# A hybrid decoder layer: Delta-net masks and scalings moved from POOL to DVE, small inverse products spaced out, a weight load moved ahead of the masks

## The chip, the cores and the metric

The kernel runs on one core of one Trainium2 chip. The metric is the device time of one execution in microseconds (us). Three timed executions of the kernel before gave a median of 1263.71 us (1262.24 to 1264.34). The engines are called as in the profile: PE (matrix products; PEld is its weight load), DVE (vector), ACT (scalar and activations), POOL (the third elementwise engine), SP (here it only issues transfers).

## The reference

One decoder layer over 16 meta tokens and 256 tokens, width 2048, in float32. The input goes through an RMS norm and one combined projection. Half of its columns feed a differential attention, the other half a gated Delta net; both results are concatenated, projected back and added; then comes a SwiGLU feed-forward of hidden width 5632. The part that matters here is the Delta net, in chunks, for each of 8 heads:

```python
diff = gc[..., :, None] - gc[..., None, :]
decay = jnp.where(incl, jnp.exp(jnp.where(incl, diff, 0.0)), 0.0)
kb = kc * bc[..., None]
lmat = jnp.where(strict, jnp.einsum('bhnid,bhnjd->bhnij', kb, kc) * decay, 0.0)
tmat = lmat + jnp.eye(CHUNK, dtype=f32)
u = lax.linalg.triangular_solve(tmat, vc * bc[..., None], left_side=True, lower=True,
                                unit_diagonal=True)
qk = jnp.einsum('bhnid,bhnjd->bhnij', qc, kc) * decay
...
o = rmsnorm(o, o_norm_w) * jax.nn.silu(z.reshape(B, L, DN_HEADS, DN_DV).astype(f32))
```

`decay` is the exponential of a difference of running sums of the gates, masked to a triangle; the key products are scaled by `bc` (beta and the key norms) and by the decay; a unit triangular matrix is inverted for each head.

## The kernel before, in words

**Weights.** Every weight matrix streams from HBM as tiles of 128 x 1024 floats (`raw`, 512 KB, four buffers). Each is split by ACT into a rounded part `hi` (line 250) and by DVE into the remainder `lo` (line 251); each has four buffers. The products then run in a fast format as `hi*xh + hi*xl + lo*xh` (line 1086 in the input projection, 24 products per tile; line 1133 afterwards). `next_w` splits four tiles ahead and asks for loads three further. The input itself is split the same way at the start, into `xh` (ACT, line 325) and `xl` (DVE, line 326), 16 slices of 128 x 272, with the first weight tiles split between the slices.

**Side work.** `proj` emits the weight products in groups of six and, after each group, `tasks.step()` advances up to two of the waiting generators (`decay`, `conv_task`, `unit`, `inverses`, `attention` ...). A generator's `yield n` postpones it by n such steps. So the distance of two pieces of side work on PE is written in steps, not in time. ACT and SP run their instructions in the order in which they are emitted; on PE, DVE and POOL a scheduler puts them in order, by its own estimate of times, when the program is built. Once built, every engine takes its instructions strictly in that order. PSUM tiles of the side work come from a ring of four (`aux`), so the fifth user waits until the first is read.

**The Delta net.** `meta_block` treats the 16 meta positions of all heads as one 128 x 128 block; `unit(g, n)` treats four heads of one of two 128-position chunks (four units). Each starts with `decay`: a mask times the gates (line 475, POOL), products with a triangle (line 479, PE), an exponential (ACT), a mask (line 485, POOL). When the key scalars `c1` (line 573) and `c2` (line 574) are there, POOL scales the decay by `c1` (line 792) and DVE multiplies it with the key products of line 795 into `gT` (line 798; line 735 for the meta block). The keys are scaled by `c2` on POOL (line 815). `inverses(n)` inverts the triangles: it sends `gT` through DRAM, runs a recursion on 16 x 16 blocks on DVE (lines 630, 631), fetches the result, and joins blocks to 32, 64 and 128 with small PE products (lines 663, 677: 32 products of 32 x 16, or 16 of 32 x 32, on parts of the PE array). For that POOL masks `gT` into `gm` (line 624). `meta_block` then makes the first state: line 749 transposes the values (PE), line 753 scales them (DVE), line 763 multiplies them by the inverse (PE), line 759 scales keys for eight heads (POOL), line 772 makes the state (PE). `z_task` applies the SiLU gate (ACT) and the output norm weight (line 911, POOL).

**The key path early on.** `conv_task` scales a finished projection (line 502, DVE), convolves it (line 511 on ACT, three passes of line 514 on DVE per head) and applies SiLU (ACT) into `k_c`, `v_c`, `q_c`. `sums` transposes the keys on PE (line 539).

Of the kernel before, what the change touches and what calls it, by code (L numbers as in the profile page):

```python
# [15 lines left out]
P = 128  # L16
# [139 lines left out]
def layer(tc, xT, aw, x, w_in, w_ba, w_out, w_gate, w_up, w_down, cmask, dist, par, out):  # L156
# [122 lines left out]
        elif i in (3, 5, 7):  # L279
            load_to((i + 1) // 2)  # L280
    wba_raw = wk.tile([P, KT, WBA], F32, name="wba_raw")
    nc.sync.dma_start(out=wba_raw, in_=w_ba)
    cmsk = const.tile([P, len(CM), P], F32, name="cmsk")
    nc.sync.dma_start(out=cmsk, in_=cmask)
    par_sb = const.tile([P, NPAR], F32, name="par_sb")
    nc.sync.dma_start(out=par_sb, in_=par)
    dist_sb = wk.tile([P, META + P + T], F32, name="dist_sb")

    def pr(n):
# [33 lines left out]
    for k in range(KT):  # L323
        src, w = xr[k // 8][:, k % 8, :], aw_sb[:, k:k + 1]
        S.activation(xh[:, k, :], src, AF.Copy, scale=w)
        V.scalar_tensor_tensor(xl[:, k, :], src, w, xh[:, k, :], ALU.mult, ALU.subtract)  # L326
        if k == 0:
            split_to(1, 2)
        elif k in (5, 9, 13):
            split_to((k + 3) // 4)  # L330


    rbc = const.tile([P, T], F32, name="rbc")
# [138 lines left out]
    def decay(u, gcols, tri, m, dst):  # L472
        yield at_least("ga", 1)
        gt = yield from r2.get(m, P)
        G.tensor_tensor(gt, bc_mid(mk("tri_s"), m), bc_last(gcols, P), ALU.mult)
        yield 3
        ps = yield from aux.get(m, P)
        for h in range(m):
            PE.matmul(ps[:, h, :], gt[:, h, :], mk("tri_i"), start=True, stop=True)
        r2.free()  # L480
        yield 1
        act(dst, ps, AF.Exp)
        aux.free()
        yield 1
        G.tensor_tensor(dst, dst, bc_mid(tri, m), ALU.mult)
        mark("decay")


# [44 lines left out]
    ktm = {}  # L533
# [71 lines left out]
    def inverses(n):  # L605

        m0, m = (0, 9) if n == 0 else (9, 8)
        f = slice(1 + 8 * n, 9 + 8 * n)
        q = 8 * m
        yield at_least(f"gT{n}", 3 - n)
        gT, y, gm = big_tile("gT"), big_tile("y"), big_tile("gm")
        d = dpool.tile([m, PLANE], F32, tag=f"d{n}", name=f"d{n}")
        nc.sync.dma_start(out=d[:, 0:P * P].rearrange("m (r c) -> r m c", c=P), in_=gT[:, m0:m0 + m, :])
        gb = (yield from r1.get(16, 16))[0:q]
        nc.sync.dma_start(out=gb, in_=bass.AP(d.tensor, d.offset, [[PLANE // 8, q], [P, 16], [1, 16]]))  # L620
        yt = yield from r1.get(256)
        V.memset(yt, 0.0)
        V.memset(yt[:, 0:256:17], 1.0)
        G.tensor_tensor(gm[:, f, :], gT[:, f, :], bc_mid(mk("off16"), 8), ALU.mult)
        yb = yt[0:q].rearrange("p (r i) -> p r i", i=16)
        tb = (yield from r1.get(16, 16))[0:q]
        yield 14
        for i in range(1, 16):
            t = tb[:, 0:i, 0:i]
            V.tensor_tensor(t, yb[:, 0:i, 0:i], bc_mid(gb[:, 0:i, i], i), ALU.mult)  # L630
            V.tensor_reduce(yb[:, 0:i, i], t, AX.X, ALU.add, negate=True)  # L631
            if i > 4:
                yield 3
        V.tensor_copy(tb, yb.rearrange("p r i -> p i r"))
        e = dpool.tile([q, 256], F32, tag=f"e{n}", name=f"e{n}")
        nc.sync.dma_start(out=e, in_=tb.rearrange("p i r -> p (i r)"))
        x16 = yield from r1.get(m, 16)
        nc.sync.dma_start(out=x16, in_=bass.AP(e.tensor, e.offset, [[16, P], [2048, m], [1, 16]]))
        r1.free(3)
        yield 14  # L640
        x32 = yield from r2.get(m, 32)
        V.tensor_scalar(x32[:, :, 0:16], x16, pr("lo16"), None, ALU.mult)
        V.tensor_scalar(x32[:, :, 16:32], x16, pr("hi16"), None, ALU.mult)
        r1.free()
        y32 = yield from r2.get(m, 32)
        V.transpose(y32, x32)
        if n == 0:
            expand(y[:, 0:1, :], y32[:, 0:1, :], 1, 32, mk("bd32"))
            mark("inv_m")
        yield 2  # L650
        if n == 0:
            x32, y32 = x32[:, 1:9, :], y32[:, 1:9, :]
        gT, y, gm = gT[:, f, :], y[:, f, :], gm[:, f, :]
        a_ = yield from r2.get(8, 64)
        for w in (16, 32):

            parts = [(32 * b, 32 * b) for b in range(4)] if w == 16 else [(0, 32), (64, 96)]
            src = gm if w == 16 else gT
            ps = yield from aux.get(8, w)

            for h in range(8):
                for r0, c0 in parts:
                    PE.matmul(ps[c0:c0 + 32, h, :], src[r0:r0 + 32, h, c0:c0 + 32], x32[r0:r0 + 32, h, 0:w],
                              start=True, stop=True, tile_position=(r0, c0))
            yield 2
            a = a_[:, :, 0:w]
            if w == 16:
                S.copy(a, ps)
            else:
                for _, c0 in parts:  # L670
                    S.copy(a[c0:c0 + 32], ps[c0:c0 + 32])
            aux.free()
            yield 1
            ps = yield from aux.get(8, w)
            for h in range(8):
                for _, c0 in parts:
                    PE.matmul(ps[c0:c0 + 32, h, :], y32[c0:c0 + 32, h, :], a[c0:c0 + 32, h, :],
                              start=True, stop=True, tile_position=(c0, c0))
            yield 2
            if w == 16:  # L680
                V.tensor_tensor(x32[:, :, 0:16], x32[:, :, 0:16], ps, ALU.subtract)
                aux.free()
                V.transpose(y32, x32)
                yield 2
        x64 = a_
        for b in range(4):
            bs = slice(32 * b, 32 * b + 32)
            if b % 2:
                V.tensor_scalar(x64[bs, :, 0:32], ps[bs], -1.0, None, ALU.mult)
            else:  # L690
                G.tensor_copy(x64[bs, :, 0:32], x32[bs])
        aux.free()
        V.tensor_scalar(x64[:, :, 32:64], x32, pr("hi32"), None, ALU.mult)
# [24 lines left out]
        yield 2  # L718
        S.activation(y[0:64, :, 64:128], ps[0:64], AF.Copy, scale=-1.0)
        aux.free()  # L720
        r2.free(2)
        mark("inv")
        mark(f"inv{n}")

    state = wk.tile([P, H, P], F32, tag="state", name="state")
    def meta_block():
# [28 lines left out]
        for g in range(2):  # L755
            t = yield from r2.get(4, P)
            ksm.append(t)
            for h in range(4):
                G.tensor_scalar(t[:, h, :], ktm["m"], c2m[:, 4 * g + h:4 * g + h + 1], None, ALU.mult)
        aux.free()  # L760
        yield 1
        ps = yield from aux.get(1, P)
# [17 lines left out]
    def unit(g, n):  # L780
# [8 lines left out]
        yield from decay(u, ga[:, cs], mk("tri_i"), 4, dq)  # L789
        yield at_least("c1", 1)  # L790
        kc = qkv["k"]
        G.tensor_tensor(dq, dq, bc_last(c1[:, cs], P), ALU.mult)
        ps = yield from aux.get(4, P)
        for i, h in enumerate(hs):
            PE.matmul(ps[:, i, :], kc[:, h, ts_], kc[:, h, ts_], start=True, stop=True)
        yield 3
        yield 1
        V.tensor_tensor(dt, ps, dq, ALU.mult)
        aux.free()
        yield 1  # L800
        mark(f"gT{n}")
# [10 lines left out]
        aux.free()  # L812
        if n == 0:
            ks = ktm[g]
            G.tensor_tensor(ks, ks, bc_last(c2[:, cs], P), ALU.mult)
        yield at_least(f"state{g}", n + 1)
        ps = yield from aux.get(4, P)
        for i, h in enumerate(hs):
# [24 lines left out]
        for i, h in enumerate(hs):  # L843
            PE.matmul(ps[:, i, :], kc[:, h, ts_], qc[:, h, ts_], start=True, stop=True)
        yield 1
        V.tensor_tensor(dq, ps, dq, ALU.mult)
        aux.free()
        if n == 0:
            ps = yield from aux.get(4, P)
# [35 lines left out]
        r2.free()  # L885
        yield 1
        val = yield from r2.get(4, P)
        V.tensor_tensor(val, ps, sz[:, 4 * g:4 * g + 4, P * n:P * (n + 1)], ALU.mult)
        aux.free()
        yield at_least("chain", 4)  # L890
        for part in ("hi", "lo"):
# [11 lines left out]
    def z_task(h, ps):  # L903
# [2 lines left out]
        V.tensor_tensor(z, ps[:, 0:SEQ], rbc[:, META:T], ALU.mult)  # L906
        mm.free()
        yield 1
        act(z, z, AF.Silu)
        yield 1  # L910
        G.tensor_scalar(sz[:, h, :], z, pr("onorm"), None, ALU.mult)
        r1.free()
        mark("z")

# [419 lines left out]
```

## Time and profile before

| what | value |
|---|---|
| median of 3 timed runs | 1263.71 us (1262.24 to 1264.34) |
| the profiled execution's own time | 1262.79 us |
| its span, first to last instruction | 1261.0 us |
| PE busy | 1244.4 us (99%) |
| DVE busy | 729.4 us (58%), 1084 instructions |
| ACT busy | 610.9 us (48%) |
| POOL busy | 46.8 us (4%), 48 instructions |
| PE clock granted, mean | 0.996 |

The busy times are sums over instructions as the profiler saw them; a PE product that waits inside the pipeline counts as busy, so PE's 99% does not say that PE ran at its best speed throughout. The idle times that the profile lists before each instruction, with what ended them, say where PE stood still. Windows of the span show each engine's busy time and the clock granted to PE in that stretch: 1.00 is full speed, 0.50 half. Times of single instructions are from their start to their end; where instructions of one engine overlap in its pipeline, a row of n of them is shorter than n times one.

### The profile page before, as it was taken

Reading aid. Unit: us, or ns where it says so; the run is one execution under the profiler, and the core shown is the slowest. Engines: PE = TensorE matmul, PEld = TensorE weight load, DVE = VectorE, ACT = ScalarE, POOL = GpSimd, SP = SyncE. Lnnn points to the kernel's source line nnn. Section 1 sums busy time; section 2 is a strip of 40 time slices with the busy share of each in tenths; the row PEclk is TensorE's granted clock in tenths of the full one; section 3 lists DMA queues with packets and bytes.
Section 4 is the critical chain, followed back from the end, with each engine's and each line's share of the span. In section 5 each row is a group of like instructions: output and inputs, shape, how many; then the busy total and the mean of one; then the engine's idle time right before and its main releaser. Section 6 shows DMA issues by size and latency. Waiting matters only on the chain.

```text
span 1261.0 us, 18878 instructions
## 1 busy us (share of the span) xinstructions
PE 1244.4 (99%) x7469; PEld 1092.2 (87%) x7469; DVE 729.4 (58%) x1084; ACT 610.9 (48%) x962; POOL 46.8 (4%) x48
## 2 busy tenths in 40 slices
PE   8999999999999999999999999999999999999998
PEld 7998989999999988888888888888888888888886
DVE  7789956567676666645544554554455454544443
ACT  6664454466776655544344444444444433343332
POOL 0322200110000000000000000000000000000000
PEclk9999999999999999999999999999999999999999
DMA  8456642345544655566665566556666555656562
GB/s 270 134 168 176 179 138 85 118 151 167 158 144 151 218 167 183 177 194 191 190 190 190 187 192 192 184 186 198 185 189 194 187 191 190 215 189 213 191 210 83
DMA packets 150280, 224.31 MB, mean 178 GB/s; under 512 B 11560, under 2 KB 72368, under 8 KB 149936
## 3 DMA queue, kind: packets, MB, share of 16 engines
q1 hardware_dynamic: 150192, 223.11, 55.8%
q8 instruction: 58, 0.95, 0.3%
q14 instruction: 30, 0.25, 0.1%
HBM read 219.73 MB, written 3.35 MB: 177 GB/s over the span
## 4 chain that ended last, share of the span: by engine, by line
PE 89%; DVE 6%; ACT 2%; DMA 1%; issue 1%; SPq 0%; DVEq 0%; ACTq 0%
PE mm L1133 64%; PE mm L1086 19%; DVE lo L251 2%; DVE r L514 1%; DMA raw<-in_w_in_dram 1%; PE aux L1216 1%; PE aux L1034 1%; ACT hi L250 1%; PE aux L989 1%; DVE r L630 0%; PE aux L1021 0%; PE aux L381 0%; SPq L276 0%; DVE r L631 0%; DMA e<-r 0%
## 5 line engine op out<-in xcount | busy, mean ns | idle before, releaser
L251 DVE TENSOR_TENSOR lo<-raw,hi 128x1024 fp32r<-128x1024 f32 (+1 forms) x409 | 504.9, 1236 | 469.5 <-ACT hi L250 468.4
L250 ACT CAST hi<-raw 128x1024 fp32r<-128x1024 f32 (+1 forms) x409 | 428.8, 1050 | 546.7 <-PE mm L1133 447.7
L1133 PE MATMUL mm<-hi,uh 128*128 128x512 f32 x704 | 274.9, 390 | 0.0
L1133 PE MATMUL mm<-hi,ul 128*128 128x512 f32 x704 | 274.0, 389 | 0.0
L1133 PE MATMUL mm<-lo,uh 128*128 128x512 f32 x704 | 273.9, 389 | 0.0
L1086 PE MATMUL mm<-xh,hi 128*128 128x272 f32 (+2 forms) x896 | 260.7, 291 | 1.6 <-ACT hi L250 1.6
L1086 PE MATMUL mm<-xh,lo 128*128 128x272 f32 (+2 forms) x896 | 255.6, 286 | 3.0 <-issue 1.8
L1086 PE MATMUL mm<-xl,hi 128*128 128x272 f32 (+2 forms) x896 | 256.7, 287 | 0.0
L1133 PE MATMUL mm<-hi,hT 128*128 128x512 f32 x704 | 217.2, 389 | 0.0
L1086 PEld LDWEIGHTS mm<-xh,hi 128*128 128x128 f32 x896 | 169.6, 189 | 5.8 <-issue 3.0
L1086 PEld LDWEIGHTS mm<-xh,lo 128*128 128x128 f32 x896 | 168.8, 189 | 1.9 <-DVE lo L251 1.9
L1086 PEld LDWEIGHTS mm<-xl,hi 128*128 128x128 f32 x896 | 169.3, 189 | 0.3 <-DVE xl L326 0.2
L1133 PEld LDWEIGHTS mm<-hi,ul 128*128 128x128 f32 x704 | 132.1, 188 | 27.6
L1133 PEld LDWEIGHTS mm<-hi,hT 128*128 128x128 f32 x704 | 132.1, 188 | 27.3
L1133 PEld LDWEIGHTS mm<-hi,uh 128*128 128x128 f32 x704 | 132.2, 188 | 27.1
L1133 PEld LDWEIGHTS mm<-lo,uh 128*128 128x128 f32 x704 | 132.2, 188 | 27.0
L1133 PE MATMUL mm<-lo,hT 128*128 128x512 f32 x352 | 136.9, 389 | 0.0
L1133 PEld LDWEIGHTS mm<-lo,hT 128*128 128x128 f32 x352 | 66.1, 188 | 13.7
L514 DVE SCALAR_TENSOR_TENSOR r<-r,par_sb,r 128x272 f32<-128x272 f32 (+1 forms) x72 | 34.7, 541 | 0.2 <-ACT r L511 0.2
L1133 PE MATMUL mm<-hi,mix_d_hi 128*128 128x512 f32 x64 | 25.5, 399 | 0.0
L1133 PE MATMUL mm<-hi,mix_a_hi 128*128 128x512 f32 x64 | 25.1, 392 | 0.0
L1133 PE MATMUL mm<-hi,mix_d_lo 128*128 128x512 f32 x64 | 25.0, 390 | 0.0
(305 smaller groups left out, 849.8 us busy)
## 6 DMA issues: line engine op xcount, KB each, us to landing
raw<-in_w_in_dram SPq DMA_DIRECT2D x111, 512.0 KB, 3.6
raw<-in_w_gate_dram SPq DMA_DIRECT2D x88, 512.0 KB, 3.5
raw<-in_w_up_dram SPq DMA_DIRECT2D x88, 512.0 KB, 3.5
raw<-in_w_down_dram SPq DMA_DIRECT2D x88, 512.0 KB, 3.5
raw<-in_w_out_dram SPq DMA_DIRECT2D x32, 512.0 KB, 3.5
xr<-in_xT_dram SPq DMA_DIRECT2D x7, 272.0 KB, 6.0
x_k_c<-in_x_dram SPq DMA_DIRECT2D x1, 1024.0 KB, 6.5
x_q_c<-in_x_dram SPq DMA_DIRECT2D x1, 1024.0 KB
```

What stands on the lines that cost most here:

```text
L250: S.copy(hi[:, js], raw[:, js])
L251: V.tensor_tensor(lo[:, js], raw[:, js], hi[:, js], ALU.subtract)
L514: V.scalar_tensor_tensor(acc, raw[:, off + j:off + j + m], cwv[:, ct, j:j + 1], acc, ALU.mult, ALU.add)
L989: PE.matmul(pss[m][:, cut[n]], q[ms, P * n:P * (n + 1)], k[ms, 0:NK[n]], start=True, stop=True)
L1034: PE.matmul(po[:, n, :], l, r, start=(j == 0), stop=(j == 1 + n))
L1086: PE.matmul(acc[c][:, 0:n], a[:, k, cs], b[:, kt, t0:T], start=(kt == 0 and i == 0), stop=(kt == KT - 1 and i == 2))
L1133: PE.matmul(acc[b], l, r[:, i % 2, :], start=(first and i == 0 and j == 0), stop=(last and i == len(kts) - 1 and j == 2))
L1216: PE.transpose(pst[:, j, :], g_[:, P * j:P * (j + 1)], ident)
```

## The change

1. `decay`: the mask times gates (line 475) becomes one `tensor_scalar` per head on DVE, 17 of them of 128 x 128; the mask after the exponential (line 485) goes from POOL to DVE as it is.
2. `unit`: the scaling of the decay by `c1` (line 792, POOL) goes. Instead `c1` is folded into the two products that use the decay (lines 798 and 846): each DVE instruction over 128 x 512 becomes four over 128 x 128 with three operands.
3. `inverses`: the mask of line 624 goes to DVE. The waits between the small products grow from 2, 1 and 2 steps to 5, 3 and 5.
4. Key scaling: line 759 goes to DVE as it is (eight instructions); line 815 becomes eight instructions of 128 x 128 on DVE.
5. `z_task` writes the SiLU straight to `sz`; the output norm weight of line 911 moves into the later product of line 888.
6. At the start, the first tiles are split in two halves each, one input slice earlier, and the fifth weight tile's load is issued ahead of the loads of `w_ba`, the masks (640 KB) and the parameters.

```diff
     wba_raw = wk.tile([P, KT, WBA], F32, name="wba_raw")
-    nc.sync.dma_start(out=wba_raw, in_=w_ba)
     cmsk = const.tile([P, len(CM), P], F32, name="cmsk")
-    nc.sync.dma_start(out=cmsk, in_=cmask)
     par_sb = const.tile([P, NPAR], F32, name="par_sb")
-    nc.sync.dma_start(out=par_sb, in_=par)
...
         if k == 0:
             split_to(1, 2)
-        elif k in (5, 9, 13):
-            split_to((k + 3) // 4)
+            load_to(5)
+            for dst, src in ((wba_raw, w_ba), (cmsk, cmask), (par_sb, par)):
+                nc.sync.dma_start(out=dst, in_=src)
+        elif k in (4, 8, 12):
+            split_to(k // 4 + 1, 2)
+            load_to(k // 4 + 5)
...
-        G.tensor_tensor(gt, bc_mid(mk("tri_s"), m), bc_last(gcols, P), ALU.mult)
+        for h in range(m):
+            V.tensor_scalar(gt[:, h, :], mk("tri_s"), gcols[:, h:h + 1], None, ALU.mult)
...
-        G.tensor_tensor(dst, dst, bc_mid(tri, m), ALU.mult)
+        V.tensor_tensor(dst, dst, bc_mid(tri, m), ALU.mult)
...
-        G.tensor_tensor(gm[:, f, :], gT[:, f, :], bc_mid(mk("off16"), 8), ALU.mult)
+        V.tensor_tensor(gm[:, f, :], gT[:, f, :], bc_mid(mk("off16"), 8), ALU.mult)
...
-            yield 2
+            yield 5
             a = a_[:, :, 0:w]
...
-            yield 1
+            yield 3
             ps = yield from aux.get(8, w)
...
                 V.transpose(y32, x32)
-                yield 2
+                yield 5
...
-                G.tensor_scalar(t[:, h, :], ktm["m"], c2m[:, 4 * g + h:4 * g + h + 1], None, ALU.mult)
+                V.tensor_scalar(t[:, h, :], ktm["m"], c2m[:, 4 * g + h:4 * g + h + 1], None, ALU.mult)
...
-        G.tensor_tensor(dq, dq, bc_last(c1[:, cs], P), ALU.mult)
...
-        V.tensor_tensor(dt, ps, dq, ALU.mult)
+        for i in range(4):
+            V.scalar_tensor_tensor(dt[:, i, :], ps[:, i, :], c1[:, cs][:, i:i + 1], dq[:, i, :], ALU.mult, ALU.mult)
...
-            G.tensor_tensor(ks, ks, bc_last(c2[:, cs], P), ALU.mult)
+            for i in range(4):
+                V.tensor_scalar(ks[:, i, :], ks[:, i, :], c2[:, cs][:, i:i + 1], None, ALU.mult)
...
-        act(z, z, AF.Silu)
-        yield 1
-        G.tensor_scalar(sz[:, h, :], z, pr("onorm"), None, ALU.mult)
+        act(sz[:, h, :], z, AF.Silu)
```

The product of line 846 (`qkT`) is split into four like that of line 798, and that of line 888 gets the norm weight as a third operand.

The scheduler puts PE's and DVE's instructions in a new order in three places that matter below. In the listings, `L` is the source line (from line 281 on, a line of the changed kernel differs by a few from that of the kernel before: 1086 is 1087, 539 is 541, 479 is 481, 663 is 665, 677 is 679, 763 is 765, 753 is 755), then the operation, out<-in, and the size of the result.

PE, early in the key path. `L539` are the key transposes of `sums`, two heads at a time, into two PSUM tiles; `L1086` are weight products. Before:

```order
L539 MATMUL aux_749<-cmsk,k_c 128x128 x2
L1086 MATMUL mm_615<-xh,hi_567 128x272
...
L539 MATMUL aux_730<-cmsk,k_c 128x128
L539 MATMUL aux_749<-cmsk,k_c 128x128
```

Now:

```order
L541 MATMUL aux_767<-cmsk,k_c 128x128 x2
L1087 MATMUL mm_633<-xh,hi_573 128x272
...
L1087 MATMUL mm_633<-xh,hi_635 128x272
L541 MATMUL aux_748<-cmsk,k_c 128x128
L541 MATMUL aux_767<-cmsk,k_c 128x128
```

Between the transposes of the first two heads and those of the next two there were four weight products; now there are 19.

DVE, where the meta block's first state is prepared. `L753` scales the transposed values, `L514` is the convolution, `L681` belongs to the small inverse products. Before:

```order
L514 SCALAR_TENSOR_TENSOR r_54_1989<-r_52_1979,par_sb,r_54_1989 128x256
L251 TENSOR_TENSOR lo_2004<-raw_1901,hi_2003 128x1024
L753 TENSOR_SCALAR r_56_2105<-aux_2096,ksq 128x128
L251 TENSOR_TENSOR lo_2085<-raw_1931,hi_2084 128x1024
L681 TENSOR_TENSOR r_16_2015<-r_16_2015,aux_2117 128x8x16
```

Now:

```order
L516 SCALAR_TENSOR_TENSOR r_54_2015<-r_52_2005,par_sb,r_54_2015 128x256
L251 TENSOR_TENSOR lo_2030<-raw_1927,hi_2029 128x1024
L761 TENSOR_SCALAR r_21_2132<-ktm_m,c2m 128x128 x4
L761 TENSOR_SCALAR r_22_2137<-ktm_m,c2m 128x128 x4
L755 TENSOR_SCALAR r_56_2130<-aux_2122,ksq 128x128
L251 TENSOR_TENSOR lo_2111<-raw_1957,hi_2110 128x1024
```

The eight key scalings (line 759 before, 761 now) stand ahead of the scaling of the values.

PE, at the small inverse products (`L663`, `L677`; x32 is one group) and the meta block's products. Before:

```order
L663 MATMUL aux_2036<-r_16_2015,gm 32x16 x32
...
L749 MATMUL aux_2096<-cmsk,r_55_2075 128x128
...
L677 MATMUL aux_2117<-r_18_2035,r_17_2018 32x16 x32
...
L763 MATMUL aux_2156<-r_56_2105,y 128x128
L663 MATMUL aux_2159<-r_19_2079,gm 32x16 x32
...
L772 MATMUL aux_2214<-r_57_2198,r_21_2107 128x128 x4
```

Now:

```order
L665 MATMUL aux_2062<-r_16_2041,gm 32x16 x32
...
L751 MATMUL aux_2122<-cmsk,r_55_2101 128x128
...
L665 MATMUL aux_2143<-r_19_2105,gm 32x16 x32
...
L765 MATMUL aux_2182<-r_56_2130,y 128x128
...
L774 MATMUL aux_2205<-r_57_2190,r_21_2132 128x128 x4
L541 MATMUL aux_2210<-cmsk,q_c 128x128 x4
...
L679 MATMUL aux_2244<-r_18_2061,r_17_2044 32x16 x32
```

The dots are weight products. Three groups of 32 small products stood before the state products of line 772 (774 now). Now two stand there, and the third comes after them, 24 weight products and both halves of the state later than the product of line 763.

More of the change, by code (lines that the diff above doesn't have):

```diff
@@ L795, in unit @@
             PE.matmul(ps[:, i, :], kc[:, h, ts_], kc[:, h, ts_], start=True, stop=True)
-        yield 3
-        yield 1
-        V.tensor_tensor(dt, ps, dq, ALU.mult)
+        yield 4
+        for i in range(4):
+            V.scalar_tensor_tensor(dt[:, i, :], ps[:, i, :], c1[:, cs][:, i:i + 1], dq[:, i, :], ALU.mult, ALU.mult)
         aux.free()
@@ L845, in unit @@
         yield 1
-        V.tensor_tensor(dq, ps, dq, ALU.mult)
+        for i in range(4):
+            V.scalar_tensor_tensor(dq[:, i, :], ps[:, i, :], c1[:, cs][:, i:i + 1], dq[:, i, :], ALU.mult, ALU.mult)
         aux.free()
@@ L887, in unit @@
         val = yield from r2.get(4, P)
-        V.tensor_tensor(val, ps, sz[:, 4 * g:4 * g + 4, P * n:P * (n + 1)], ALU.mult)
+        V.scalar_tensor_tensor(val, ps, pr("onorm"), sz[:, 4 * g:4 * g + 4, P * n:P * (n + 1)], ALU.mult, ALU.mult)
         aux.free()
@@ L908, in z_task @@
         yield 1
-        act(z, z, AF.Silu)
-        yield 1
-        G.tensor_scalar(sz[:, h, :], z, pr("onorm"), None, ALU.mult)
+        act(sz[:, h, :], z, AF.Silu)
         r1.free()
```

## The prediction

> **What bounds the kernel now.** I read the page's totals first, then the chain that ended last. The first row of the next fence is the span, the second PE's total, the third the chain by engine.
>
> ```profile
> span 1261.0 us, 18878 instructions
> PE 1244.4 (99%) x7469; PEld 1092.2 (87%) x7469; DVE 729.4 (58%) x1084; ACT 610.9 (48%) x962; POOL 46.8 (4%) x48
> PE 89%; DVE 6%; ACT 2%; DMA 1%; issue 1%; SPq 0%; DVEq 0%; ACTq 0%
> ```
>
> PE sets the end. Its products stay the same in number and size, so only time in which PE stands still, or runs at half clock, can be won. The list of PE's waits, grouped by what ended them, gives the places that this change can touch.
>
> ```profile
> PE aux L795 <- DVE gT L735: 3.1, 1, 3.1
> PE mm L1086 <- issue: 1.8, 1, 1.8
> PE aux L539 <- ACT k_c L196: 1.7, 1, 1.7
> PE mm L1086 <- ACT hi L250: 1.6, 2, 0.9
> ```
>
> Then I cut the span into windows around these waits: length, busy time (and instructions) of PE, PEld, DVE, ACT and POOL, granted clock, DMA share, GB/s.
>
> ```profile
> 9.10:12.40 3.30, 1.85 (x13) 1.43 (x12) 1.91 (x3) 2.62 (x5) 0.00 (x0) 1.00 1.06 380
> 89.20:161.20 72.00, 68.93 (x611) 68.50 (x609) 69.44 (x156) 32.73 (x46) 21.39 (x21) 0.98 0.61 175
> 95.30:98.30 3.00, 0.00 (x0) 0.00 (x0) 3.00 (x5) 0.67 (x2) 0.88 (x1) 0.91 0.00 0
> 98.40:101.10 2.70, 2.70 (x12) 2.70 (x13) 2.70 (x5) 1.02 (x2) 1.60 (x1) 0.50 0.87 263
> 162.70:166.00 3.30, 1.69 (x72) 1.46 (x71) 0.68 (x2) 0.27 (x1) 0.78 (x2) 1.00 0.90 286
> 166.20:169.40 3.20, 3.20 (x16) 3.20 (x16) 1.23 (x1) 1.21 (x2) 0.00 (x0) 0.50 0.04 12
> ```
>
> Two readings. After the waits at 95 and at 164 the clock is 0.50 for about 3 us, although PE is busy: a stall there is paid again, with half of 2.70 = 1.35 us and half of 3.20 = 1.6 us. It did not follow at 9.1, where PE was idle for 3.30 - 1.85 = 1.45 us, and it did at 162.7, with 1.61 idle. And DVE is busy for 69.44 of 72 us between 89 and 161: there the second engine has no room.
>
> **The first tiles.** Three more splits in halves cost ACT time: two halves take 1.34 us, one whole 1.05.
>
> ```profile
> 4.75 1.34 ACT L250 CAST hi<-raw 128x512 fp32r<-128x512 f32 x2 [0.30 <-DMA raw<-in_w_in_dram]
> 17.45 2.28 ACT L340 ACTIVATE r<-xr 128x544 f32<-128x544 f32 x4
> 20.50 1.05 ACT L250 CAST hi<-raw 128x1024 fp32r<-128x1024 f32 x1 [0.76 <-DVE lt L426]
> 24.59 0.40 ACT L375 CAST wba<-wba_raw 128x256 fp32r<-128x256 f32 x1
> ```
>
> A first half is ready 1.05 - 0.67 = 0.38 us sooner, at the two waits for `hi` of the list; against that stand 0.29 us more of ACT time for each split. I take 0.2 us gained. The fifth tile's earlier load gives nothing: its split at 20.50 stands behind ACT's own queue (line 340), not behind a DMA. On SP the masks, `w_ba` and parameters go behind 512 KB, an estimated 1.4 us at the 380 GB/s of the 9.1 row; `w_ba` is first used at 24.59 with no wait for it. If that cover fails, up to 1.4 is lost; from a clock drop there about the same, and at best I see 0.5 gained.
>
> **The wait at 52.5.** POOL's masks (line 475) leave; 17 instructions go to DVE, ahead of the split and of the convolution for which `k_c` waits.
>
> ```profile
> 40.43 0.17 DVE L404 COPY ga<-bat 128x16 f32<-128x16 f32 x1
> 40.51 0.17 DVE L405 COPY gb<-bat 128x16 f32<-128x16 f32 x1
> 46.23 0.18 DVE L449 SCALAR_TENSOR_TENSOR ga<-ga,t 128x17 f32<-128x17 f32 x1
> 46.49 5.38 POOL L475 TENSOR_TENSOR r<-cmsk,ga 128x128 f32<-128x128 f32 x5 [46.06 <-DVE ga L449]
> 50.89 3.54 DVE L514 SCALAR_TENSOR_TENSOR r<-r,par_sb,r 128x272 f32<-128x272 f32 x6
> 66.27 2.55 DVE L514 SCALAR_TENSOR_TENSOR r<-r,par_sb,r 128x272 f32<-128x272 f32 x6
> 54.53 0.44 PE L539 MATMUL aux<-cmsk,k_c 128*128 128x128 f32 x2 [1.72 <-ACT k_c L196]
> 203.50 1.90 DVE L822 SCALAR_TENSOR_TENSOR r<-aux,ne_gc,r 128x128 f32<-128x128 f32 x7
> 160.89 0.34 DVE L753 TENSOR_SCALAR r<-aux,ksq 128x128 f32<-128x128 f32 x1
> ```
>
> While POOL works, DVE's instructions are longer: six of line 514 take 3.54 us against 2.55 in the later row. A `tensor_scalar` of 128 x 128 with POOL idle is not in the trace. Bounds, start to start: 0.08 us (lines 404 to 405, 16 columns) and 1.90/7 = 0.27 (line 822, the same size with two operands, one in PSUM); above that 0.34, start to end of line 753. I take 0.18, midway between the first two. So DVE ends line 514 at 46.41 + 17 x 0.18 + 0.2 (line 466) + 1.2 (line 251) + 2.55 = 53.4 us instead of 54.4. The second transposes of line 539 move behind 15 more weight products; products stand 68.93/611 = 0.113 us apart on average in the 89.2 row, so 1.7 us. PE gets there at 52.8 + 1.7 - 0.2 = 54.3 instead of 54.53 - 1.72 = 52.8, later than `k_c` is ready. The wait of 1.7 goes, 1.8 us with its restart; at 0.27 DVE ends at 54.9 and 0.7 of it is lost. The mask of line 485 adds five DVE instructions, four of 128 x 512 of which none costs more than a split's 1.2 us; DVE waits for ACT there:
>
> ```profile
> 57.77 1.48 DVE L251 TENSOR_TENSOR lo<-raw,hi 128x1024 fp32r<-128x1024 f32 x1 [2.21 <-ACT hi L250]
> ```
>
> Its cover is that idle time; without it a few us of DVE come due in the stretch from 89 on.
>
> **The wait at 95.** The fourth unit's products need the PSUM tile that line 735 reads.
>
> ```profile
> 89.43 4.36 POOL L792 TENSOR_TENSOR qkT<-qkT,c 128x512 f32<-128x512 f32 x4 [10.76 <-DVE c L573]
> 89.61 1.01 DVE L574 TENSOR_TENSOR c<-c,eg 128x17 f32<-128x17 f32 x1
> 90.55 1.13 DVE L731 TENSOR_SCALAR gT<-gT,c 128x128 f32<-128x128 f32 x1
> 91.60 4.88 DVE L514 SCALAR_TENSOR_TENSOR r<-r,par_sb,r 128x272 f32<-128x272 f32 x4
> 97.95 0.28 DVE L735 TENSOR_TENSOR gT<-aux,gT 128x128 f32<-128x128 f32 x1
> ```
>
> Line 514 took 4.88 us for four, at the pace of 66.27 1.7; lines 574 and 731 took 2.14, by the rows of lines 449 and 753 about 0.54. That is 3.2 + 1.6 = 4.8 us, more than the wait of 3.1, and line 735 moves up with it. The wait goes, and the half clock: 3.1 + 1.35 = 4.4 us (3.1 to 4.6).
>
> **The wait at 164.** Nothing that the profile shows held PE here. What remains is instruction supply: the DMA view for 152.9 to 163.9 has no line of the instruction queue q8; for 163.9 to 166.1 it has the first of these rows. The second is the page's for the whole span.
>
> ```profile
> q8 instruction: 1, 0.02, 2.7%
> q8 instruction: 58, 0.95, 0.3%
> 166.19 0.38 PE L1086 MATMUL mm<-xh,lo 128*128 128x260 f32 x1 [1.80 <-issue]
> ```
>
> One block is 0.95 MB/58 = 16 KB. Three groups of 32 small products run here in quick succession, and weight loads go with them, so PE uses up instructions much faster than among weight products; the next block came too late. With the waits of 5, 3 and 5 steps one group moves behind the state products. I take the stall and its half clock as gone: 1.8 + 1.6 = 3.4 us (0 to 3.4). The Trainium skill, "Runtime: NRT & Kernel Launch", section "Instruction fetch mechanics", says that instructions come in blocks of 256 (16 KiB), fetched while the current one runs, and that crossing a block's end is mostly hidden; by that the stall is something else, or spacing won't move it, and the sum below would be smaller by the 3.4 us. The trace agrees on the block's size and not, here, on the hiding; that it doesn't go is a rival.
>
> **The new wait, at line 763.** Before line 753 DVE now has eight key scalings of line 759 and more. What POOL's work cost DVE between 89 and 161 comes back:
>
> ```profile
> L251 DVE TENSOR_TENSOR lo<-raw,hi 128x1024 fp32r<-128x1024 f32 x21 | 29.2, 1392 | 0.5 <-ACT hi L250 0.5
> L798 DVE TENSOR_TENSOR gT<-aux,qkT 128x512 f32<-128x512 f32 x4 | 2.6, 676 | 0.0
> 159.76 1.21 DVE L251 TENSOR_TENSOR lo<-raw,hi 128x1024 fp32r<-128x1024 f32 x1
> 162.92 0.38 PE L763 MATMUL aux<-r,y 128*128 128x128 f32 x2
> ```
>
> Back: 21 x (1.39 - 1.22) = 3.6, and the 4.8 above, so 8.4 us. Added: 16 of 128 x 128 for line 798, 16 x 0.27 - 2.6 = 1.7; line 624 twice, near a split's 1.2 each, 2.4; lines 759 and 815, 16 x 0.18 = 2.9: 7.0 us. DVE also starts 2.0 us earlier, with PE. Line 753 ended at 160.89 + 0.34 = 161.23; now at 161.23 - 2.0 - 8.4 + 7.0 = 157.8 us, but PE is there at 162.92 - 0.2 - 1.8 - 4.4 = 156.5. PE waits about 1.4 us (0 to 4), and behind it in its queue stand weight products that could run. By the rows of 9.1 and 162.7 an idle 1.4 us doesn't halve the clock; 1.6 would, for 1.5 us more.
>
> The other parts I cost at nothing: lines 846, 888 and 911 come after 163, where DVE's 58% of the span leaves room. If not, line 888 costs a few tenths.
>
> **Sum.** 0.2 + 1.8 + 4.4 + 3.4 - 1.4 = 8.4 us. From the profiled execution's 1262.8 (span 1261.0) that is 1254.4. The median of the runs is 0.9 above that execution: **1255.3 us**. About 0.2% (2.5 us) is what a measurement of this kernel can tell from no change.
>
> **The rivals.**
>
> *The fetch stall stays, or moves to the next groups.* Two groups still stand before line 763, as close as before. 8.4 - 3.4 = 5.0 us gained, 1258.7. Against it: one group fewer in the critical 4 us.
>
> *No new wait at line 763.* If the small DVE instructions cost 0.08 and not 0.18, the 16 save 1.6 us, more than the wait of 1.4. Gain 9.8 us, 1253.9.
>
> *DVE as a wall.* At 0.30 us for each small instruction (near line 753's row) line 514 ends at 55.5 and, with 0.1 to the products, 1.3 of the 1.8 us are lost; at line 763 16 x 0.12 + 16 x 0.03 = 2.4 us are added, and the half clock's 1.5. Gain 8.4 - 1.3 - 2.4 - 1.5 = 3.2 us, 1260.5. With the fetch stall left as well, it is 0.2 us slower, 1263.9: the case of no change.
>
> *Slower: the moved instructions cost DVE what they cost POOL.* The place is the queue ahead of line 753, and that of `k_c`.
>
> ```profile
> L759 POOL TENSOR_SCALAR r<-ktm_m,c2m 128x128 f32<-128x128 f32 x8 | 6.3, 803 | 0.0
> ```
>
> Each 0.01 us more costs 17 + 32 = 49 of them 0.49 us, since both places are waited for. From 0.30 on it takes 3.2/49 = 0.07 us to reach zero: from 0.37 us on the kernel is slower; at 0.45, still well below that row's 0.80, 1260.5 + 49 x 0.15 = 1267.9. Against it: no DVE row of that size with POOL idle is above 0.34, even from start to end.
>
> **How the numbers follow.** The forecast 0.60; the fetch stall stays 0.12; no new wait 0.08; the wall 0.12; these are faster by over 0.2%: 0.92. Wall and fetch stall together, no change: 0.05. Slower 0.03. The range goes from 1251.0 (no new wait, 0.5 us more at the start, and up to 2.4 from small waits that I left out, line 884's 0.7 among them) to 1261.0, just past the wall.
>
> **What would show it.** Right: no wait of PE at line 795 for line 735, none by issue near 160, no clock of 0.50 between 95 and 170, line 514 six in 2.6 us at 50, lines 477 and 761 at 0.18 us a piece, a wait of 1 to 2 us at line 765 for line 755. Wrong: line 477 over 0.27 us; a q8 packet with PE idle behind it; a wait of over 3 us at 765; the half clock at a new place, at the start above all; or line 251 still at 1.39 us between 89 and 161 with POOL idle.

## The result and the profile after

| | before | changed |
|---|---|---|
| median of the runs, us | 1263.9 (1262.24 to 1264.34, 4 runs) | 1255.13 (1253.01 to 1255.81, 4 runs) |
| ratio, with its 95% interval | 1 | 0.993 (0.9913 to 0.9947) |
| profiled execution, its span, us | 1262.79, 1261.0 | 1253.01, 1251.2 |

The changed kernel is 8.8 us faster (0.7%). The forecast was 1255.3. Its terms did not all come out, though: the new wait was worse than forecast, the three stalls that went were worth more, and these partly cancelled. The profiled execution of the changed kernel was also the quickest of its four, and one term can't be seen in it at all; the first experiment shows it.

The page of the changed kernel, the same three rows as before: span, busy times, chain by engine.

```profile
span 1251.2 us, 18894 instructions
PE 1243.1 (99%) x7469; PEld 1090.8 (87%) x7469; DVE 731.3 (58%) x1151; ACT 610.6 (49%) x965; POOL 5.3 (0%) x14
PE 97%; DMA 1%; ACT 1%; DVE 1%; SPq 0%; issue 0%; DVEq 0%
```

DVE fell from 6% of the chain to 1%, though it has 67 instructions more. POOL's 46.8 us became 5.3. Now PE's waits, the whole list:

```profile
PE aux L269 <- DVE r L503: 1.2, 1, 1.2
PE mm L1087 <- DVE lo L251: 1.0, 2, 0.8
PE mm L1087 <- ACT hi L250: 0.8, 1, 0.8
PE aux L887 <- DVE r L883: 0.4, 1, 0.4
PE mm L1087 <- DVE xl L323: 0.2, 1, 0.2
```

The waits for `k_c` (1.7), for line 735 (3.1) and by issue (1.8) are gone. So is the forecast's new wait at line 765, here. In windows (length; busy time and instructions of PE, PEld, DVE, ACT, POOL; clock; DMA share; GB/s) the long stretch is now full, but the start has a half clock that it did not have before:

```profile
20.20:23.50 3.30, 1.79 (x13) 1.36 (x12) 3.20 (x6) 3.30 (x7) 0.00 (x0) 1.00 1.09 348
23.60:26.90 3.30, 3.30 (x16) 3.30 (x16) 3.30 (x7) 1.64 (x3) 0.00 (x0) 0.50 0.71 218
86.80:157.00 70.20, 70.20 (x692) 69.86 (x691) 68.69 (x190) 34.18 (x48) 3.21 (x5) 1.00 0.64 186
```

Between 86.8 and 157 PE is busy for 70.20 of 70.20 us at full clock; before it was 68.93 of 72.00. DVE's side, the timeline and then the groups of 86.8 to 157:

```profile
48.02 3.42 DVE L477 TENSOR_SCALAR r<-cmsk,ga 128x128 f32<-128x128 f32 x17
52.57 2.56 DVE L516 SCALAR_TENSOR_TENSOR r<-r,par_sb,r 128x272 f32<-128x272 f32 x6
88.97 1.73 DVE L516 SCALAR_TENSOR_TENSOR r<-r,par_sb,r 128x272 f32<-128x272 f32 x4
92.17 0.28 DVE L737 TENSOR_TENSOR gT<-aux,gT 128x128 f32<-128x128 f32 x1
146.63 0.36 DVE L644 TENSOR_SCALAR r<-r,par_sb 128x144 f32<-128x144 f32 x1 [0.90 <-DMA r<-e]
155.32 1.66 DVE L761 TENSOR_SCALAR r<-ktm_m,c2m 128x128 f32<-128x128 f32 x8
156.89 0.35 DVE L755 TENSOR_SCALAR r<-aux,ksq 128x128 f32<-128x128 f32 x1
```

```profile
L251 DVE TENSOR_TENSOR lo<-raw,hi 128x1024 fp32r<-128x1024 f32 x22 | 26.6, 1212 | 0.2
L799 DVE SCALAR_TENSOR_TENSOR gT<-aux,c,qkT 128x128 f32<-128x128 f32 x16 | 4.3, 329 | 0.0
L626 DVE TENSOR_TENSOR gm<-gT,cmsk 128x1024 f32<-128x1024 f32 x2 | 2.4, 1213 | 0.0
```

A small `tensor_scalar` costs 3.42/17 = 0.20 and 1.66/8 = 0.21 us (0.18 was taken). Line 516 is back at 2.56 for six and 1.73 for four, line 251 at 1.21, and line 737 ends at 92.4 instead of 98.2.

### The profile page after: what moved, and what is told of

The parts are those of the page before. It is cut to its first block, busy times and chain, and to the rows that moved or that the text cites. A ratio compares the mean times of both kernels' runs of the same rounds, so it can differ in the third digit from the quotient of the medians.

```text
span 1251.2 us, 18894 instructions
## 1 busy us (share of the span) xinstructions
PE 1243.1 (99%) x7469; PEld 1090.8 (87%) x7469; DVE 731.3 (58%) x1151; ACT 610.6 (49%) x965; POOL 5.3 (0%) x14
## 4 chain that ended last, share of the span: by engine, by line
PE 97%; DMA 1%; ACT 1%; DVE 1%; SPq 0%; issue 0%; DVEq 0%
PE mm L1134 64%; PE mm L1087 25%; PE aux L1217 1%; PE aux L1035 1%; DMA raw<-in_w_in_dram 1%; PE aux L990 1%; DMA xr<-in_xT_dram 0%; PE aux L1022 0%; PE aux L382 0%; PE aux L481 0%; PE aux L838 0%; PE aux L846 0%; PE aux L821 0%; PE aux L864 0%; PE aux L830 0%; PE aux L796 0%
## 5 line engine op out<-in xcount | busy, mean ns | idle before, releaser
L251 DVE TENSOR_TENSOR lo<-raw,hi 128x1024 fp32r<-128x1024 f32 (+1 forms) x412 | 499.0, 1213 | 456.2 <-ACT hi L250 455.9
L516 DVE SCALAR_TENSOR_TENSOR r<-r,par_sb,r 128x272 f32<-128x272 f32 (+1 forms) x72 | 30.9, 485 | 0.2 <-ACT r L513 0.2
```

The lines of the kernel that those rows point to most:

```text
L251: V.tensor_tensor(lo[:, js], raw[:, js], hi[:, js], ALU.subtract)
L516: V.scalar_tensor_tensor(acc, raw[:, off + j:off + j + m], cwv[:, ct, j:j + 1], acc, ALU.mult, ALU.add)
```

## The experiments

The theory was the forecast's: three separate stalls of PE go, each for its own part of the change, and DVE's longer queue costs a wait at line 765. The runs came in three groups, r0 to r3, r4 to r7 and r8 to r11, each timed on a chip of its own beside the kernel before (1264.13, 1264.12 and 1263.73 us). So differences between groups, such as r4 against r0 or r8 against r6, are across chips, and a few tenths of them may be the chip. Line numbers shift by one in some kernels.

**r0: the changed kernel again.**

> The changed kernel again, for comparison with its variants on one chip. If the half clock at 23.6 us belongs to the new start, it is there again and the median is near 1255. If it was chance (the input landed 0.9 us late in that execution), the clock is 1.00 there and the median 1253.5 or so.

Measured: 1256.03 us (1251.19 to 1256.55, 6 runs), 0.9927 of before (0.9913 to 0.994). The half clock at 23.6 is not there, and yet the execution is 3 us longer than the first one. Its list of waits, its timeline (DVE, then PE) and two windows:

```profile
PE aux L765 <- DVE r L755: 2.7, 1, 2.7
```

```profile
147.99 0.36 DVE L644 TENSOR_SCALAR r<-r,par_sb 128x144 f32<-128x144 f32 x1 [3.11 <-DMA r<-e]
158.24 0.35 DVE L755 TENSOR_SCALAR r<-aux,ksq 128x128 f32<-128x128 f32 x1
158.65 0.49 PE L765 MATMUL aux<-r,y 128*128 128x128 f32 x2 [2.75 <-DVE r L755]
```

```profile
155.70:158.50 2.80, 0.20 (x2) 0.00 (x0) 2.80 (x10) 1.31 (x2) 0.00 (x0) 1.00 0.49 135
159.60:163.00 3.40, 3.40 (x19) 3.40 (x18) 1.35 (x2) 1.05 (x2) 0.00 (x0) 0.50 0.62 178
```

This is the new wait, twice the forecast's size, and its half clock. What differs between two executions of one program is upstream, and there are two things. The first is on DVE: line 644 waits 3.11 us for the result of the inverses that comes back through DRAM, 0.90 in the first execution. The DMA view of 143 to 149 gives that transfer from issue to landing, first in the first execution, then here:

```profile
r<-e SPq DMA_DIRECT2D x1, 72.0 KB, 2.3
```

```profile
r<-e SPq DMA_DIRECT2D x1, 72.0 KB, 4.2
```

Everything that DVE does after line 644 moves with it, line 755 too: it ends at 158.59 here and at 157.24 in the first execution, 1.35 us apart. The second is on PE, which comes earlier: the wait begins at 158.65 - 2.75 = 155.90, while the first execution starts this product at 157.29, 1.4 us later, with no wait. That lateness is there at the second transposes of line 541 already (first the first execution, then r0). It comes from the first execution's start: its first weight product is 0.6 us later, and the half clock at 23.6 adds the rest:

```profile
55.93 0.38 PE L541 MATMUL aux<-cmsk,k_c 128*128 128x128 f32 x2
```

```profile
54.49 0.38 PE L541 MATMUL aux<-cmsk,k_c 128*128 128x128 f32 x2
```

So each of the two makes up about half of the 2.75 us. Four of the six runs lie between 1256.0 and 1256.6, the other two at 1251.2 and 1253.0. One of the four was profiled and has the wait; the first execution, at 1253.01, has not. The two quick runs have no trace.

**r1: spacing undone in the changed kernel.**

```diff
-            yield 5
+            yield 2
             a = a_[:, :, 0:w]
...
-            yield 3
+            yield 1
             ps = yield from aux.get(8, w)
...
-                yield 5
+                yield 2
```

> Only the waits between the small products go back to 2, 1 and 2 steps. Theory (they use up a block of instructions faster than the next one comes): PE waits 1.8 us by issue behind the third group, near 156, and runs 3.2 us at half clock after that; 3.4 us slower than the changed kernel, 1258.5. Rival (the stall hung on the moment, and any shift of PE by 6 us removes it): no wait by issue, 1255.

Measured: 1257.54 us (1257.2 to 1258.76), 1.5 slower than r0. The wait by issue is back, but smaller than the theory had it; the larger wait is another:

```profile
PE aux L679 <- ACT r L670: 2.5, 1, 2.5
PE mm L1087 <- issue: 0.8, 1, 0.8
```

Close together, the second group of small products waits for ACT's copy of the first one's result. The wait at 765 is not in the list: PE stood still before it. So the 1.5 us are what is left of both waits and their half clock after r0's 2.7 and its half clock have gone.

**r2: spacing alone, in the kernel before.**

```diff
-            yield 2
+            yield 5
             a = a_[:, :, 0:w]
...
-            yield 1
+            yield 3
             ps = yield from aux.get(8, w)
...
-                yield 2
+                yield 5
```

> The kernel before with only the waits of 5, 3 and 5 steps. Theory: the wait by issue at 164 and its half clock go, the waits at 52.5 and 95 stay; 1263.9 - 3.4 = 1260.5. Rival (spacing doesn't help, POOL's removal does): 1263.9, with the wait by issue there or at a later group.

Measured: 1259.4 us (1259.2 to 1259.84), 4.7 less than before, where 3.4 was expected. The waits at 52 and 95 stand as they were, none by issue, and the stretch of the old stall is full:

```profile
PE aux L795 <- DVE gT L735: 3.1, 1, 3.1
PE aux L539 <- ACT k_c L196: 1.7, 1, 1.7
```

```profile
155.00:170.00 15.00, 15.00 (x300) 14.50 (x300) 9.33 (x17) 8.91 (x26) 0.00 (x0) 1.00 0.81 247
```

The rival, that POOL's removal did it, falls. The 4.7 is not all spacing, though. The two profiled executions differ by 1262.79 - 1259.84 = 2.95 us only, since that of the kernel before was 1.3 quicker than its median; between the same two weight products on either side of the stall (the 900th and the 3000th), the two traces differ by 3.6 us, near the 3.4 of the forecast.

**r3: the old start in the changed kernel.**

```diff
             split_to(1, 2)
-            load_to(5)
-            for dst, src in ((wba_raw, w_ba), (cmsk, cmask), (par_sb, par)):
-                nc.sync.dma_start(out=dst, in_=src)
-        elif k in (4, 8, 12):
-            split_to(k // 4 + 1, 2)
-            load_to(k // 4 + 5)
+        elif k in (5, 9, 13):
+            split_to((k + 3) // 4)
```

(The three loads stand behind their tiles again, as before.)

> The changed kernel with the start of the kernel before (whole splits, fifth tile's load behind the masks). Theory (the forecast): the new start is worth 0.2 us, so 1255.3. Rival (the new start lets PE run ahead, which puts two waits into one stretch and halves the clock): no 0.50 before 90 us, 1253.6, 1.5 us faster than the changed kernel.

Measured: 1255.42 us (1253.02 to 1257.12). The runs spread over 4 us, so this settles nothing; r8 tells more.

**r4: the scaling by c1 on POOL again.**

```diff
+        G.tensor_tensor(dq, dq, bc_last(c1[:, cs], P), ALU.mult)
...
-        for i in range(4):
-            V.scalar_tensor_tensor(dt[:, i, :], ps[:, i, :], c1[:, cs][:, i:i + 1], dq[:, i, :], ALU.mult, ALU.mult)
+        V.tensor_tensor(dt, ps, dq, ALU.mult)
```

(The product of line 849 likewise.)

> The changed kernel with the scaling of the decay by c1 on POOL again (and the two products that use it over 128 x 512). Theory: four POOL instructions of 1.1 us from 88 on make DVE's line 516 and line 733 slower by about 4 us, line 737 comes late, PE waits 2 to 3 us at line 796 and its clock halves; 1259 to 1260. Rival (the wait at 95 went because of the order, or of line 817): no wait at 796, 1256.

Measured: 1256.92 us (1256.06 to 1258.44), 0.9 above r0. The mechanism is the one named; its price is smaller. POOL and DVE in the timeline, and PE's list of waits:

```profile
86.31 4.71 POOL L794 TENSOR_TENSOR qkT<-qkT,c 128x512 f32<-128x512 f32 x4 [9.48 <-DVE c L575]
```

```profile
87.63 4.10 DVE L516 SCALAR_TENSOR_TENSOR r<-r,par_sb,r 128x272 f32<-128x272 f32 x4
```

```profile
PE aux L765 <- DVE r L755: 2.1, 1, 2.1
PE aux L797 <- DVE gT L737: 1.4, 1, 1.4
```

Four of line 516 take 4.10 us instead of 1.73, and PE waits 1.4 us, without a half clock behind it. Before, with line 815 on POOL too, it was 4.88 and a wait of 3.1. The wait at 765 is 2.1 instead of r0's 2.7: part of the loss is taken back there, so 0.9 is less than the wait at 797 costs by itself.

**r5: the first mask on POOL again.**

```diff
-        for h in range(m):
-            V.tensor_scalar(gt[:, h, :], mk("tri_s"), gcols[:, h:h + 1], None, ALU.mult)
+        G.tensor_tensor(gt, bc_mid(mk("tri_s"), m), bc_last(gcols, P), ALU.mult)
```

> The changed kernel with the first mask (line 477) on POOL again; the transposes of line 541 stand 4 products apart again. Theory: DVE's six of line 516 take 3.5 us, PE waits 1.7 us for k_c; 1256.0 + 1.8 = 1257.8. Rival (a loss ahead of the wait at 765 is swallowed by it): the wait at 52 is there, and the one at 765 shorter by as much, 1256.

Measured: 1257.75 us (1257.13 to 1258.23), 1.7 above r0, as the theory had it. In the timeline the six of line 516 (515 here) are slow again, and the list of waits has both of PE's. The rival has a small part in it, 2.4 at line 764 instead of r0's 2.7. The order of the transposes came back with the mask, so the two aren't told apart:

```profile
49.97 4.12 DVE L515 SCALAR_TENSOR_TENSOR r<-r,par_sb,r 128x272 f32<-128x272 f32 x6
```

```profile
PE aux L764 <- DVE r L754: 2.4, 1, 2.4
PE aux L540 <- ACT k_c L196: 1.4, 1, 1.4
```

**r6: the product of line 765 later.**

```diff
         aux.free()
-        yield 1
+        yield 5
         ps = yield from aux.get(1, P)
         PE.matmul(ps[:, 0, :], y[:, 0, :], r, start=True, stop=True)
```

> The changed kernel with the product of line 765 four steps later on PE, DVE's order as it is. Theory: the wait of 2.7 us and the half clock behind it go; 1256.0 - 4.2 = 1251.8, and the runs no longer spread over 5 us, since the landing of the fetch of line 640 doesn't reach PE any more. Rival (the next step is as late: state products, small products): a wait of 2 us or more shows up at 774 or 679, 1255 or so.

Measured: 1252.09 us (1251.88 to 1252.26), 0.9904 of before (0.9889 to 0.9919), 3.9 less than r0, and the runs spread over 0.4 us. Between the 900th and the 3000th weight product the traces of r0 and r6 differ by 4.7 us, the wait and its half clock; r6's execution gave 0.5 back at the start, where its clock halved and r0's did not. DVE still waits for the same transfer (timeline), and PE doesn't notice (window):

```profile
148.39 0.36 DVE L644 TENSOR_SCALAR r<-r,par_sb 128x144 f32<-128x144 f32 x1 [2.84 <-DMA r<-e]
```

```profile
26.90:200.00 173.10, 173.10 (x1770) 170.12 (x1769) 141.71 (x361) 103.94 (x201) 5.08 (x10) 1.00 0.57 163
```

**r7: the key scalings twice.**

```diff
                 V.tensor_scalar(t[:, h, :], ktm["m"], c2m[:, 4 * g + h:4 * g + h + 1], None, ALU.mult)
+                V.tensor_scalar(t[:, h, :], ktm["m"], c2m[:, 4 * g + h:4 * g + h + 1], None, ALU.mult)
```

> The changed kernel with each key scaling of line 761 done twice; nine of the sixteen and one split now stand ahead of line 755, one instruction and one split more than before. Theory (DVE's queue decides when 765 starts): line 755 ends 0.2 + 1.15 = 1.35 us later, PE's wait there grows from 2.7 to 4.0, 1257.4. Rival (PE's wait there has another cause than what stands in DVE's queue): unchanged, 1256.

Measured: 1257.71 us (1257.39 to 1257.92), 1.7 above r0. The wait (line 766 here) grew by 1.3 us, as DVE's queue says:

```profile
PE aux L766 <- DVE r L755: 4.0, 1, 4.0
```

**r8 to r11: four variants of r6,** whose narrow spread makes one microsecond easier to read.

r8 has r3's edit on top of r6's.

> The kernel with the later product of line 765 (1252.1), with the start of the kernel before. There the runs spread over 0.4 us only, so the start can be read. Theory (the forecast: the new start is worth 0.2 us): 1252.3. Rival (its half clock at 23.5, seen in two of the profiled executions, belongs to it): 1250.6, with 1.00 from 7 to 90.

Measured: 1251.03 us (1250.94 to 1251.16), 0.9895 of before (0.9881 to 0.991), 1.06 less than r6 (0.7 less if each is taken against the kernel before on its own chip). In r6 the stretch behind the waits at 20 and 22 runs at half clock; in r8 the clock is full (windows of r6, then of r8):

```profile
23.50:26.80 3.30, 3.30 (x17) 3.30 (x16) 3.30 (x7) 0.77 (x2) 0.00 (x0) 0.50 0.56 176
```

```profile
7.00:158.00 151.00, 148.30 (x1304) 145.54 (x1304) 137.97 (x356) 93.86 (x171) 3.51 (x6) 1.00 0.66 194
```

So the new start lost time here, together with the half clock. But that half clock is not in every execution with the new start: of the nine profiled ones (the first, r0, r1, r4 to r7, r9, r10) three have it, the first, r6 and r9. PE reaches the second transposes of line 541 at 55.93, 54.97 and 55.17 in these three; at 53.80 to 54.52 in r0, r1, r4, r7 and r10, where the clock stayed full; and with the old start at 54.13 (r3) and 54.25 (r8). Without the half clock, then, the two starts are alike. Why it falls in some executions and not in others was left open.

r9 has r1's edit on top of r6's.

> The kernel with the later product of line 765, and the waits between the small products back at 2, 1 and 2. Theory (instruction supply): PE waits by issue, 0.8 to 1.8 us, behind the groups of small products, with a half clock behind it; 1254 to 1255.5. Rival (what spacing saves is the wait of line 679 for ACT's copies, 2.5 us and a half clock): that wait is there, none by issue over 0.3 us, 1256. If neither is there, spacing isn't needed: 1252.

Measured: 1257.87 us (1257.13 to 1258.08), 5.8 above r6. Both waits are there, and half clock for 6.7 us from behind the first one on (list of waits, timeline, window):

```profile
PE aux L679 <- ACT r L670: 2.6, 1, 2.6
PE mm L1087 <- issue: 1.2, 1, 1.2
```

```profile
162.88 0.38 PE L1087 MATMUL mm<-xh,hi 128*128 128x260 f32 x1 [1.21 <-issue]
```

```profile
159.50:166.20 6.70, 5.49 (x90) 5.13 (x79) 2.88 (x8) 1.21 (x2) 0.79 (x2) 0.50 0.56 168
```

Its DMA view has one q8 line in 159 to 161 and none in 161 to 163; PE starts again at 162.88, after it. So it was before: the packet in 163.9 to 166.1, PE again at 166.19. By the packets' own times in the traces, the packet landed 1.3 us before PE went on in the kernel before, 1.2 us in r1 and 1.4 us in r9. The page counts 58 such packets for PE's 7469 products and 7469 weight loads, one for every 258 of them, so q8 very likely feeds PE, though the profile doesn't say whose instructions a packet holds. A group of small products counts 64 products and 64 weight loads in 0.7 us here (line 679), half a packet; weight products, 0.113 us apart by the prediction's row, take about 7 us for as many.

r10 puts three of the moved parts back on POOL, on top of r6.

```diff
-        V.tensor_tensor(gm[:, f, :], gT[:, f, :], bc_mid(mk("off16"), 8), ALU.mult)
+        G.tensor_tensor(gm[:, f, :], gT[:, f, :], bc_mid(mk("off16"), 8), ALU.mult)
...
-                V.tensor_scalar(t[:, h, :], ktm["m"], c2m[:, 4 * g + h:4 * g + h + 1], None, ALU.mult)
+                G.tensor_scalar(t[:, h, :], ktm["m"], c2m[:, 4 * g + h:4 * g + h + 1], None, ALU.mult)
...
-            for i in range(4):
-                V.tensor_scalar(ks[:, i, :], ks[:, i, :], c2[:, cs][:, i:i + 1], None, ALU.mult)
+            G.tensor_tensor(ks, ks, bc_last(c2[:, cs], P), ALU.mult)
```

> The kernel with the later product of line 765, and lines 626, 761 and 817 on POOL again, as in the kernel before; the first mask, c1 and the exponential's mask stay on DVE. Theory (only what ends in a wait of PE counts, and these don't): 1252.1, within 0.5. Rival (12 us of POOL slow DVE's line 251 to 1.4 us and bring a wait at 765 or at a weight tile): 1254 or more.

Measured: 1252.43 us (1251.86 to 1252.97), 0.3 above r6, which looks like nothing. But the half clock of r6's start was not there in its profile, and the granted clock is 1.000 in all five of its runs, 0.998 in all four of r6. PE reaches the second transposes of line 541 at 54.52, 0.45 us ahead of r6 (54.97), and line 765's product at 160.34, 0.37 behind it (159.97). In between 0.8 us were lost, where a wait of 0.6 came at line 796, against the theory. Line 816 (815 before, 817 in the changed kernel) runs on POOL beside DVE's line 516, four of which take 3.34 us instead of 1.73 (timeline, then list of waits):

```profile
87.53 2.24 POOL L816 TENSOR_TENSOR r<-r,c 128x512 f32<-128x512 f32 x2 [9.99 <-DVE c L576]
87.55 3.34 DVE L516 SCALAR_TENSOR_TENSOR r<-r,par_sb,r 128x272 f32<-128x272 f32 x4
```

```profile
PE aux L796 <- DVE gT L737: 0.6, 1, 0.6
```

By its place in time the loss is line 815's, worth about 0.8 us at the wait at 95. No wait of PE came with lines 626 and 761 back on POOL.

r11 delays the squares of the input norm, on top of r6.

```diff
-    tasks.spawn(input_rms(), delay=0)
+    tasks.spawn(input_rms(), delay=4)
```

> The kernel with the later product of line 765, and the squares of the input norm four steps later, so that the fifth weight tile's split doesn't stand behind four of them on ACT. Theory (ACT's queue causes the waits at 20.8 and 22.3): those 1.8 us go, and where the clock halved there, 1.6 more; 1249 to 1250.3. Rival (the norm's result, 2 to 3 us later, is waited for): a new wait between 27 and 60 takes it back, 1252 or more.

Measured: 1250.98 us (1250.8 to 1251.26), 0.9895 of before (0.9881 to 0.991), 1.1 below r6. The 1249 to 1250.3 expected were not reached. Two waits of 1.7 us together (lines 250 and 251) shrank to 1.0, one of 0.6 for `k_c` came as the rival had it, and these nearly cancel. The clock stayed at 1.00, where r6 lost half of 3.30 us, and that covers the 1.1; since r10 stayed at 1.00 with the old delay, it can't be put down to this edit. Its list of waits:

```profile
PE mm L1087 <- DVE lo L251: 0.7, 1, 0.7
PE aux L541 <- ACT k_c L196: 0.6, 1, 0.6
PE mm L1087 <- ACT hi L250: 0.3, 1, 0.3
```

r8 and r11 are the fastest of all, 4 us below the changed kernel. The two together were not run.

## Why the prediction came out, step by step

- **The first tiles: nothing gained, and about 1 us lost where the clock fell.** The forecast had 0.2 us gained; r8 against r6, which has the half clock, says 0.7 to 1.06 lost, and executions without it show neither gain nor loss. The clock drop was named as the risk and priced at about 1.4, but not put into the sum.
- **The wait at 52.5: right.** 1.8 forecast; r5 gives 1.7 back. The mask's instructions took 0.20 us for 0.18. The trace of before did have a `tensor_scalar` of 128 x 128 beside an idle POOL, line 753's own row; what it lacked was several of them in a row.
- **The wait at 95: right in effect.** Wait and half clock are gone, 4.4 us against the profile before. r4, with line 792 on POOL, brings back 1.4 us of the wait of 3.1, and r10, with line 815 on POOL, 0.6; what belongs to the order of line 796's groups on PE wasn't tried apart.
- **The wait at 164: right.** Spacing removes the wait by issue, alone (r2: 4.7 us by the medians, 3.6 in the traces, 3.4 forecast) and in the end (r9: 5.8 us). That it is worth more in the end was not seen: with PE earlier, close groups also wait 2.6 us for ACT's copies between them. In the profile before that wait isn't in the list. On the rule that the Trainium skill gives ("Runtime: NRT & Kernel Launch", section "Instruction fetch mechanics": the next block's fetch is mostly hidden), r1 and r9 decide: behind close groups of small products it was 0.8 and 1.2 us not hidden, and hidden with the groups apart.
- **The wait at 765: right in place, wrong in size.** 1.4 us without a half clock was forecast; r0 has 2.7 with one, and r6 puts both together at 3.9 us (4.7 in the traces). PE came 0.6 us earlier than forecast (155.9 for 156.5) and line 755 ended 0.8 later (158.6 for 157.8). The step that failed took DVE for busy throughout and moved line 755 up by all that POOL gave back. Part of it went into a longer idle wait for the transfer of line 640, which in r0 landed 1.8 us later after its issue than before. The timeline of before had the row that warns of it, inside a window that I had read as full:

```profile
152.03 0.36 DVE L642 TENSOR_SCALAR r<-r,par_sb 128x144 f32<-128x144 f32 x1 [1.57 <-DMA r<-e]
```

- **The sum.** 8.4 us forecast; 8.8 and, on one chip, 8.1 measured (r0). The total is better than its parts. The profiled executions of before and r0 differ by 6.7 us. To split that by place, the table takes the start of the same weight product, counted from the first, in the two traces:

| weight product | before, us | r0, us | gained since the row above | forecast |
|---|---|---|---|---|
| 200th (behind the start) | 41.26 | 41.38 | -0.1 | 0.2 |
| 400th (behind the wait at 52.5) | 74.35 | 71.97 | 2.5 | 1.8 |
| 900th (behind the wait at 95) | 145.68 | 138.66 | 4.6 | 4.4 |
| 3000th (behind 164 and line 765) | 509.54 | 503.45 | -0.9 | 3.4 - 1.4 = 2.0 |
| the end of the span | 1261.0 | 1254.3 | 0.6 | 0 |

Of the -0.9, r6, which has neither of the two waits there, puts 3.7 on the wait at 164 and -4.7 on line 765. So the forecast was 3.3 us too good at line 765 and 0.3 at the start, and 1.9 us too low elsewhere: 6.7. The remaining 1.3 of the 8.1 is that the profiled execution before lay that much under the median of 11 runs (1262.79 to 1264.13), where 0.9 was taken; why is not known. That errors of both signs came so near to 8.4 is luck.

The rival "no new wait" gives the number of the first profiled execution, but not for its reason: it took the small instructions at 0.08 us, they cost 0.20, and the wait was missing because PE came late and the transfer early. Four of r0's six runs, by the one of them that was profiled, are the forecast's case with a longer wait.

## What to carry to other kernels

Moving work off an engine that blocks another pays where a wait ends last, and only there: of the parts moved to DVE, putting one back on POOL cost 0.9 us (line 792, r4), another 1.7 (line 475, r5), a third about 0.8 (line 815, r10), each by a wait of PE; lines 624 and 759 brought no wait (r10), and line 485 was not tried. When DVE or another in-order engine gets faster, ask which transfer it will now wait for: shorter instructions don't hasten a DMA's landing, but the consumer can be put later in its own queue, as r6 did for 3.9 us with one number. An equal median can hide two effects: r10 lost 0.8 us at one place and was spared a half clock at another. And price a stall of PE with the half clock that may follow it, here 1.3 to 1.7 us more.

## What the runs showed of the hardware

- POOL's `tensor_tensor` slows DVE's instructions that run beside it: four of line 516 took 4.88, 4.10 and 3.34 us beside it (before, r4, r10), 1.73 without. Line 733's 0.28 us became 1.07 in r4.
- The same 72 KB transfer through DRAM landed 2.3 to 4.2 us after its issue, 2.3 and 4.2 in two executions of the changed kernel. What decides between them was not found.
- The clock halved after the 2.75 us stall of r0, and behind pairs of shorter waits (PE busy 1.79 of 3.30 us in the first execution), but not behind the 1.7 us wait at 52.5 of the kernel before, nor the 1.4 of r4. In the traces such a stretch lasts 3.41 us, or twice that (r1, r3, r7, r9). r0's start had nearly the same waits as the first execution's and no drop. Busy time in a window alone doesn't tell the two apart; where the rest of it lies was left open.
